# Three token-major projections by 512 columns instead of 256, the feed forward's norm spread over the output projection, and other fill orders in two stages

## The chip, the cores and the metric

The kernel runs on one core of one Trainium2 chip. The metric is the device time of one execution in microseconds (us). Before the change it is 3830.4 us, the median of 3 runs (3830.1 to 3832.64). Engines are named as the profile names them: PE is TensorE's matmul, PEld its weight load, DVE VectorE, ACT ScalarE, POOL GpSimd, SP SyncE, which issues most DMAs.

## The reference

The input is one sequence of 1024 tokens of width 1024, in fp32. Two blocks follow each other:

- The first block: a norm, one wide input projection, and four mixers of width 512 beside each other: latent attention (mla), window pooling, a state-space mixer (ssd) in 8 chunks of 128 tokens, and a linear recurrence (lru). `merged` is the sum of four gated projections of their outputs, and `x = x + merged @ w_out`. Then `x = x + square(relu(rmsnorm(x) @ w_ff1)) @ w_ff2` with 4096 hidden features, then `x = x + (p @ w_ple) * sigmoid(rmsnorm(x) @ w_ple_gate)`, and a norm.
- The second block: a modulated norm, an input projection, gated linear attention (gla) and retention, both in two directions, `x = x + mod * (mixed @ w_out_2)`, a router over 16 experts, each of which takes its best 128 tokens, the experts' feed forward, and a last norm.

In the ssd mixer, for each chunk and each of two groups g of four heads, a masked segment sum over the chunk goes through an exponential, is multiplied with the chunk's `cb` product and then with the inputs; the result is the diagonal part of the output.

## The kernel before

**Products.** Every large product is fp32 as three matmuls: operands are split into a high part (`_hi`, by ACT) and a rest (`_lo`, by DVE; `split`, L93 to L98), and `mm3` (L100 to L106) issues high by high, high by low and low by high for each block of 128 features, into one PSUM accumulator. Where the output stands token-major (128 tokens by n columns), the activations are the stationary operand and the weights stream; a name `mm<-w_hi,m_hi` in the trace is such a matmul (`m` is the merged activation, `hh` a normed one, `a` the feed forward's hidden activation).

**Weights.** `fetch` (L198) loads a weight block in two raw halves through SP's queue and splits each; the high tile and the low tile, 1 MB each, have two buffers each.

**PSUM.** Two pools: 5 accumulators for large products (`ps_mm`) and 3 for the rest (`ps_ax`).

**The order.** Each engine runs one program in order. A framework's scheduler sets it from the order of the code and from what depends on what. Where a stage has little for PE, the code takes pieces of another stage from a queue: `fill(n)` issues the next n pieces. In the ssd stage the queue holds the gate projections (`gates`): a piece there is a third of an accumulation of 24 matmuls of 512 columns, 9, 9 or 6 of them.

**The stages that the change touches:**

- ssd, L408 to L480, from about 322 to 490 us. Per chunk: 6 pieces, transposes (`s_tp`), the `cb` products, and for both groups POOL's product of the mask and the decays (`s_al`, L436), the segment sum on PE (`s_sg`, L440), the exponential on ACT (L442), the product with `cb` on DVE (`s_m`, L443) and the matmuls `s_yd` (L446). Then the off-diagonal part (`s_yo`) and the state (`s_ct`).
- the merge and `w_out`, L786 to L817, from about 1060 to 1343 us, each by halves h of 512 tokens. After a half's merged features are there, `w_out` runs in 4 blocks of 256 columns, 4 token tiles each. For h = 1, the norm of tiles 0 to 3 (`norm_half(0, g_mlp)`, L807) stands ahead of it: per tile a Square with a sum on ACT, a root, a reciprocal and a product on DVE (`n_xn`, L127), 8 transposes (`n_ps`, L117), and two splits.
- the feed forward, 1343 to 2059 us; the norm of tiles 4 to 7 stands ahead of its first group.
- the gated per-layer input (PLE), L908 to L960, 2059 to 2191 us: `w_ple_gate` in 4 blocks of 256 columns per half, beside each the product of p with `w_ple`.
- gla, where the queue gives 2 pieces before each of four states.
- `w_out_2`, L1692 to L1740, 2792 to 2916.5 us: 4 blocks of 256 columns per half; after each token tile's block DVE and POOL update x, ACT takes squares, and a routing item follows: two transposes (`q_t`, L1671), a copy on ACT (`q_xT`, L1673), two matmuls with the router (`q_lgp`, L1677). In the last block the tile's norm is written out too (`q_xn`, ACT L1689).

## Time and profile before

| what | us |
|---|---|
| median of 3 runs | 3830.4 |
| the profiled execution's own time | 3829.97 |
| its span, first to last instruction | 3828.3 |
| PE busy | 3645.7 (95%) |
| DVE busy | 2184.7 (57%) |
| ACT busy | 1595.1 (42%) |
| POOL busy | 618.8 (16%) |

The profile is of one execution. Its span leaves 1.67 us of the execution's time outside. The mean granted TensorE clock is 0.98 of 2.4 GHz; where it is 0.5 the array runs at 1.2 GHz. Matmuls are pipelined: the profile models their ends, so that the busy time of a group of matmuls counts overlap, and the pace of a stream is read from start to start.

### The profile page before, as it was taken

How to read it: one execution, taken by the hardware profiler on the slowest of the kernel's cores; microseconds unless marked ns; L12 is line 12 of the kernel's file. 1: busy time of each engine (PE TensorE's matmuls, PEld its weight loads, DVE VectorE, ACT ScalarE, POOL GpSimd, SP SyncE). 2: the span in 40 equal slices, each digit the busy share in tenths (PEclk: the TensorE clock that was granted, in tenths of full speed). 3: DMA queues.
4: the chain of work that ended last, by engine and by line, in shares of the span. 5: the costliest groups of instructions: out<-in, count | busy, mean ns of one | idle time of the engine just before them, and what ended most of it. 6: DMA issues, size and time to landing. Idle time of an engine off the chain costs nothing.

```text
span 3828.3 us, 50597 instructions
## 1 busy us (share of the span) xinstructions
PE 3645.7 (95%) x19648; PEld 3023.6 (79%) x19648; DVE 2184.7 (57%) x3304; ACT 1595.1 (42%) x2310; POOL 618.8 (16%) x731
## 2 busy tenths in 40 slices
PE   8999899999999899999999999989996999999997
PEld 6787688888779888888888988878985677777775
DVE  5425523333455566555435556575554688877777
ACT  7432243333333222222224656445242566654555
POOL 0002310101122200000000211222331222222111
PEclk9999999999999999999999999999997999999999
DMA  4211111221366423332213252223366799998987
GB/s 124 74 51 53 63 51 57 68 65 51 121 196 184 132 79 93 110 96 92 88 45 105 78 144 65 78 79 113 115 219 237 248 354 364 370 347 325 356 335 267
DMA packets 309037, 583.07 MB, mean 152 GB/s; under 512 B 27342, under 2 KB 211756, under 8 KB 308796
## 3 DMA queue, kind: packets, MB, share of 16 engines
q1 hardware_dynamic: 286508, 509.52, 39.0%
q0 software_dynamic: 22288, 70.31, 5.4%
q8 instruction: 155, 2.54, 0.3%
q14 instruction: 86, 0.70, 0.1%
HBM read 513.66 MB, written 66.09 MB: 151 GB/s over the span
## 4 chain that ended last, share of the span: by engine, by line
PE 68%; DVE 5%; issue 4%; ACT 3%; DMA 3%; POOL 2%; SPq 0%; DVEq 0%; POOLq 0%; ACTq 0%
PE mm L104 13%; PE mm L105 13%; PE mm L106 13%; PE mm L1831 5%; PE mm L1828 5%; PE mm L1829 5%; PE mm L1827 5%; PE sc L604 2%; PE m_o L638 1%; DMA w_raw<-in_w_in_dram 1%; DVE w_lo L96 1%; PE m_pt L629 1%; DMA m_g<-gates 1%; DVE e_lo L1804 1%; PE g_s L1361 1%
## 5 line engine op out<-in xcount | busy, mean ns | idle before, releaser
L104 PE MATMUL mm<-hh_hi,w_hi 128*128 128x512 f32 x1872 | 748.7, 400 | 5.4 <-ACT p_u L321 2.1
L105 PE MATMUL mm<-hh_lo,w_hi 128*128 128x512 f32 x1872 | 738.0, 394 | 0.1
L106 PE MATMUL mm<-hh_hi,w_lo 128*128 128x512 f32 x1872 | 737.1, 394 | 0.5 <-DVE w_lo L96 0.5
L1804 DVE TENSOR_TENSOR e_lo<-e_raw,e_hi 128x1408 fp32r<-128x1408 f32 (+1 forms) x308 | 502.5, 1671 | 59.2 <-ACT e_hi L1803 57.5
L96 DVE TENSOR_TENSOR w_lo<-w_raw,w_hi 128x1024 fp32r<-128x1024 f32 (+4 forms) x284 | 348.9, 1244 | 245.9 <-ACT w_hi L94 244.3
L1803 ACT ACTIVATE e_hi<-e_raw 128x1408 fp32r<-128x1408 f32 (+1 forms) x308 | 408.7, 1373 | 139.7 <-PE mm L1829 67.4
L104 PEld LDWEIGHTS mm<-hh_hi,w_hi 128*128 128x128 f32 x1872 | 354.0, 189 | 81.4 <-issue 5.1
L106 PEld LDWEIGHTS mm<-hh_hi,w_lo 128*128 128x128 f32 x1872 | 353.5, 189 | 77.6 <-issue 2.7
L105 PEld LDWEIGHTS mm<-hh_lo,w_hi 128*128 128x128 f32 x1872 | 354.3, 189 | 71.6 <-issue 3.3
L94 ACT ACTIVATE w_hi<-w_raw 128x1024 fp32r<-128x1024 f32 (+4 forms) x284 | 273.6, 985 | 326.8 <-PE mm L105 177.7
L104 PE MATMUL mm<-w_hi,hh_hi 128*128 128x256 f32 x1152 | 334.4, 291 | 0.0
L105 PE MATMUL mm<-w_lo,hh_hi 128*128 128x256 f32 x1152 | 328.5, 285 | 0.0
L106 PE MATMUL mm<-w_hi,hh_lo 128*128 128x256 f32 x1152 | 327.4, 285 | 0.0
L104 PEld LDWEIGHTS mm<-w_hi,hh_hi 128*128 128x128 f32 x1152 | 221.6, 193 | 4.1 <-issue 0.2
L105 PEld LDWEIGHTS mm<-w_lo,hh_hi 128*128 128x128 f32 x1152 | 222.0, 193 | 2.0 <-issue 1.5
L106 PEld LDWEIGHTS mm<-w_hi,hh_lo 128*128 128x128 f32 x1152 | 221.6, 193 | 0.1
L1827 PE MATMUL mm<-e_hi,e_xh 128*128 128x512 f32 x540 | 208.0, 409 | 0.0
L1828 PE MATMUL mm<-e_lo,e_xh 128*128 128x512 f32 x540 | 203.8, 377 | 0.0
L1829 PE MATMUL mm<-e_hi,e_xl 128*128 128x512 f32 x540 | 203.6, 377 | 0.0
L105 PE MATMUL mm<-w_lo,a_hi 128*128 128x512 f32 x512 | 199.6, 390 | 0.0
L104 PE MATMUL mm<-w_hi,a_hi 128*128 128x512 f32 x512 | 199.6, 390 | 0.0
L106 PE MATMUL mm<-w_hi,a_lo 128*128 128x512 f32 x512 | 199.3, 389 | 0.0
(653 smaller groups left out, 6625.4 us busy)
## 6 DMA issues: line engine op xcount, KB each, us to landing
e_raw<-in_w_exp_down_dram SPq DMA_DIRECT2D x112, 768.0 KB
e_raw<-in_w_exp_gate_dram SPq DMA_DIRECT2D x90, 704.0 KB
e_raw<-in_w_exp_up_dram SPq DMA_DIRECT2D x90, 704.0 KB
w_raw<-in_w_in_dram SPq DMA_DIRECT2D x82, 512.0 KB
w_raw<-in_w_ff_dram SPq DMA_DIRECT2D x64, 512.0 KB
w_raw<-in_w_ada_dram SPq DMA_DIRECT2D x48, 512.0 KB
e_nat<-in_w_exp_up_dram SPq DMA_DIRECT2D x32, 704.0 KB
e_nat<-in_w_exp_gate_dram SPq DMA_DIRECT2D x30, 704.0 KB
```

Source lines behind the costliest of these rows:

```text
L94: S.activation(hi, src, AF.Copy, scale=1.0 if scale is None else scale)
L96: V.tensor_sub(lo, src, hi.bitcast(F32))
L104: P.matmul(ps, ah, bh, start=start and k == 0, stop=False)
L105: P.matmul(ps, ah, bl, start=False, stop=False)
L106: P.matmul(ps, al, bh, start=False, stop=stop and k == nk - 1)
L604: P.matmul(sc[:, b:e], qT[:, h, i * 128:n], kT[:, h, b:e], start=True, stop=e < n)
L1803: S.activation(hi[:, :n], r[:, :n], AF.Copy)
L1804: V.tensor_sub(lo[:, :n], r[:, :n], hi[:, :n].bitcast(F32))
L1827: P.matmul(ps, x[0][:, k], w[0][:, c0:c1], start=k == 0, stop=False)
L1828: P.matmul(ps, x[0][:, k], w[1][:, c0:c1], start=False, stop=False)
L1829: P.matmul(ps, x[1][:, k], w[0][:, c0:c1], start=False, stop=k == last)
L1831: P.matmul(ps, x[2](k), w[:, c0:c1], start=k == 0, stop=k == last)
```

## The change

It has four parts.

1. `w_out`, `w_ple_gate` and `w_out_2` go by 512 columns. Four accumulators of 512 columns are open, one for each token tile; a weight block is 512 columns of four of the eight feature blocks (`quarter`, the same 1 MB). The first quarter passes over all four tiles, then the second one (`wide_tm`). `w_ple` goes by 512 too, and is loaded and split once instead of once per half; p's transposed form is made half by half. After a tile's second pass, x is updated by 512 columns, in PLE the squares too; in `w_out_2` the update and the routing stay at 256 columns, two after each other.
2. The feed forward's norm of tiles 0 to 3 stands inside `w_out` of h = 1 (tiles 0 and 1 behind the second pass of its first 512 columns, tiles 2 and 3 behind the first pass of the last), that of tiles 4 to 7 between the feed forward's first units.
3. In ssd the 6 pieces per chunk stand in three places: 1 ahead of the chunk, 3 between the two groups' segment sums, 2 between the two groups' `s_yd`.
4. In gla the first state of each round has 4 pieces ahead of it instead of 2.

```diff
@@ -240,6 +240,21 @@
...
     H5 = lambda h: slice(h * 512, (h + 1) * 512)
+    def quarter(w_pm, c, b):
+        return fetch(w_pm[:, b * 4:b * 4 + 4, H5(c)], 4, 512)
+    def wide_tm(w_pm, c, x, first=None):
+        ps = [ps_mm() for _ in range(4)]
+        for b in range(2):
+            w = first if first and not b else quarter(w_pm, c, b)
+            for i in range(4):
+                mm3(ps[i], x, w, 4, lambda t, k: t[:, b * 4 + k, i * 128:(i + 1) * 128], lambda t, k: t[:, k, :],
+                    start=b == 0, stop=b == 1)
+                yield i, ps[i] if b else None
@@ -406,7 +421,7 @@
...
             for c in range(NT):
-                fill(6)
+                fill(1)
                 tk = slice(c * 128, (c + 1) * 128)
@@ -430,8 +445,8 @@
...
                     S.activation(bt, p[:, :128], AF.Copy)
-                yd = ps_ax("s_yd")
-                for g in range(2):
+                def segments(g):
                     al = sp.tile([128, 2, 4, 128], F32R, name="s_al4", tag="s_xin", bufs=2)
@@ -441,9 +456,18 @@
...
                     V.tensor_mul(m, m, cbm[:, g, None, :].to_broadcast([128, 4, 128]))
+                    return m
+                yd = ps_ax("s_yd")
+                ms = [segments(0)]
+                fill(3)
+                ms.append(segments(1))
+                for g in range(2):
+                    if g:
+                        fill(2)
                     for r in range(4):
                         h = g * 4 + r
-                        P.matmul(yd[:, h * 64:(h + 1) * 64], m[:, r], xdt[:, h], start=True, stop=True)
+                        P.matmul(yd[:, h * 64:(h + 1) * 64], ms[g][:, r], xdt[:, h], start=True, stop=True)
                 y = sp.tile([128, 8, 64], F32, name="s_y", bufs=2)
@@ -804,17 +828,13 @@
...
                 hT[0] = half()
-                norm_half(0, g_mlp, range(0, 4))
-            for c in range(4):
-                w = fetch(w_out[:, :, c * 256:(c + 1) * 256], KD, 256)
-                ps = [ps_mm()[:, :256] for _ in range(4)]
-                for k0, k1 in ((0, KD - 1), (KD - 1, KD)) if c == 0 else ((0, KD),):
-                    for i in range(4):
-                        mm3(ps[i], m, w, k1 - k0, lambda t, k: t[:, k0 + k, i * 128:(i + 1) * 128],
-                            lambda t, k: t[:, k0 + k, :], start=k0 == 0, stop=k1 == KD)
-                for i in range(4):
-                    xr = xres[:, h * 4 + i, c * 256:(c + 1) * 256]
-                    V.tensor_add(xr, xr, ps[i])
+            for c in range(2):
+                for i, p in wide_tm(w_out, c, m):
+                    if p is not None:
+                        xr = xres[:, h * 4 + i, H5(c)]
+                        V.tensor_add(xr, xr, p)
+                    if h == 1 and (p is None) == (c == 1) and i % 2 == 1:
+                        norm_half(0, g_mlp, [c * 2 + i // 2])
     early.close()
@@ -857,10 +877,11 @@
...
                 w = [wf1(0), wf1(2)]
-                norm_half(1, g_mlp, range(4, 8))
-                for h in range(2):
-                    for q in range(4):
-                        act[q, h] = ff1(w[q // 2], q, h)
+                for q in range(4):
+                    act[q, 0] = ff1(w[q // 2], q, 0)
+                    norm_half(1, g_mlp, [4 + q])
+                for q in range(4):
+                    act[q, 1] = ff1(w[q // 2], q, 1)
                 fill(1)
@@ -906,19 +927,16 @@
...
     with tc.tile_pool(name="ple", bufs=1) as pl:
-        pT = (pl.tile([128, 2, T], F32R, name="pT_hi"), pl.tile([128, 2, T], F32R, name="pT_lo"))
-        pg = lambda c: fetch(w_pg[:, :, c * 256:(c + 1) * 256], KD, 256)
-        w = pg(0)
-        def ple_w(c):
-            r = pl.tile([128, 2, 256], F32, name="w2_raw", bufs=2)
-            t = pl.tile([128, 2, 256], F32R, name="w2_hi", bufs=2), pl.tile([128, 2, 256], F32R, name="w2_lo", bufs=2)
-            SP.dma_start(r, w_ple[:, :, c * 256:(c + 1) * 256])
-            split(t[0], t[1], r)
-            return t
-        w2 = ple_w(0)
-        for h in range(2):
+        w = quarter(w_pg, 0, 0)
+        w2 = pl.tile([128, 2, D], F32R, name="w2_hi"), pl.tile([128, 2, D], F32R, name="w2_lo")
+        for c in range(2):
+            r = raw_half(2, 512)
+            SP.dma_start(r, w_ple[:, :, H5(c)])
+            split(w2[0][:, :, H5(c)], w2[1][:, :, H5(c)], r)
+        def p_half(h):
+            pT = pl.tile([128, 2, 512], F32R, name="pT_hi"), pl.tile([128, 2, 512], F32R, name="pT_lo")
             pin = [pl.tile([128, 256], F32, name="p_in", bufs=4) for _ in range(4)]
@@ -926,7 +944,10 @@
...
                     P.transpose(p[:, i * 128:(i + 1) * 128], pin[i][:, j::2], ident)
-                split(pT[0][:, j, H5(h)], pT[1][:, j, H5(h)], p)
+                split(pT[0][:, j], pT[1][:, j], p)
+            return pT
+        pT = p_half(0)
         norm_half(1, g_ple, range(4, 8))
@@ -939,25 +960,23 @@
...
         for h in range(2):
-            ss = pl.tile([128, 2, 4, 4], F32, name="f_ss", bufs=2)
+            ss = pl.tile([128, 2, 4, 2], F32, name="f_ss", bufs=2)
             s1 = pl.tile([128, 2, 4], F32, name="f_s1", bufs=2)
-            for c in range(4):
-                if c or h:
-                    w, w2 = pg(c), ple_w(c)
-                for i in range(4):
-                    _, tk = tok(i)
+            if h:
+                pT = p_half(1)
+            for c in range(2):
+                for i, p in wide_tm(w_pg, c, h3[h], w if c == 0 and h == 0 else None):
+                    if p is None:
+                        continue
+                    gt = pl.tile([128, 512], F32, name="pl_g", bufs=3)
+                    S.activation(gt, p, AF.Sigmoid)
                     p = ps_mm()
-                    mm3(p[:, :256], h3[h], w, KD, lambda t, k: t[:, k, tk], lambda t, k: t[:, k, :])
-                    gt = pl.tile([128, 256], F32, name="pl_g", bufs=3)
-                    S.activation(gt, p[:, :256], AF.Sigmoid)
-                    p = ps_mm()
-                    r = slice(h * 512 + i * 128, h * 512 + (i + 1) * 128)
-                    mm3(p[:, :256], pT, w2, 2, lambda t, k: t[:, k, r], lambda t, k: t[:, k, :])
-                    V.tensor_mul(gt, p[:, :256], gt)
-                    xr = xres[:, h * 4 + i, c * 256:(c + 1) * 256]
-                    G.tensor_add(xr, xr, gt)
+                    mm3(p, pT, w2, 2, lambda t, k: t[:, k, i * 128:(i + 1) * 128], lambda t, k: t[:, k, H5(c)])
+                    V.tensor_mul(gt, p, gt)
+                    xr = xres[:, h * 4 + i, H5(c)]
+                    (V if h and c else G).tensor_add(xr, xr, gt)
                     if h == 1:
-                        squares(gt, xr, c * 256, 256, ss[:, :, i, c])
+                        squares(gt, xr, c * 512, 512, ss[:, :, i, c])
             if h == 0:
@@ -1327,7 +1346,7 @@
...
                 nla = decays(*steps[s + 1]) if s < 3 else None
-                fill(2)
+                fill(4 if s == 0 else 2)
                 states(d, h, la)
@@ -1396,7 +1415,6 @@
     w_out2 = I["w_out_2"][0].rearrange("(j p) n -> p j n", p=128)
-    wo = lambda c: fetch(w_out2[:, :, c * 256:(c + 1) * 256], KD, 256)
@@ -1512,7 +1530,7 @@
...
                     until("rg1")
-                    ahead = [wo(0), wo(1)]
+                    ahead = [quarter(w_out2, 0, b) for b in range(2)]
                     oT = [half(), half()]
@@ -1702,35 +1720,34 @@
...
         wait = []
-        for c in range(4):
-            w = ahead.pop(0) if ahead else wo(c)
-            def part(p, i, k0, k1):
-                mm3(p, oT[h], w, k1 - k0, lambda t, k: t[:, k0 + k, i * 128:(i + 1) * 128],
-                    lambda t, k: t[:, k0 + k, :], start=k0 == 0, stop=k1 == KD)
-            ps = [ps_mm()[:, :256] for _ in range(4)] if h == 0 and c == 0 else None
-            if ps:
+        for c in range(2):
+            w = ahead if ahead else [quarter(w_out2, c, b) for b in range(2)]
+            ahead = None
+            ps = [ps_mm() for _ in range(4)]
+            def part(i, k0, k1):
+                mm3(ps[i], oT[h], w[k0 // 4], k1 - k0, lambda t, k: t[:, k0 + k, i * 128:(i + 1) * 128],
+                    lambda t, k: t[:, k0 % 4 + k, :], start=k0 == 0, stop=k1 == KD)
+            split_at = (4, 7) if h == 0 and c == 0 else (4,)
+            for k0, k1 in zip((0,) + split_at[:-1], split_at):
                 for i in range(4):
-                    part(ps[i], i, 0, KD - 1)
+                    part(i, k0, k1)
             for i in range(4):
-                if ps:
-                    p = ps[i]
-                    part(p, i, KD - 1, KD)
-                else:
-                    p = ps_mm()[:, :256]
-                    part(p, i, 0, KD)
-                t = rp.tile([128, 256], F32, name="o_t", bufs=3)
-                V.tensor_mul(t, p, m2[:, c * 256:(c + 1) * 256])
-                xr = x1[i][:, c * 256:(c + 1) * 256]
-                (V if c == 3 and h else G).tensor_add(xr, xr, t)
-                S.activation(t, xr, AF.Square, accum_out=ss[:, i, c:c + 1])
-                wait.append(route(h, i, c, xr))
-                if len(wait) > 3:
-                    next(wait.pop(0))
-                if len(wait) > 2:
-                    next(wait[0])
-                if c == 3:
+                part(i, split_at[-1], KD)
+                for b in range(2):
+                    q = c * 2 + b
+                    t = rp.tile([128, 256], F32, name="o_t", bufs=3)
+                    V.tensor_mul(t, ps[i][:, b * 256:(b + 1) * 256], m2[:, q * 256:(q + 1) * 256])
+                    xr = x1[i][:, q * 256:(q + 1) * 256]
+                    (V if c and h else G).tensor_add(xr, xr, t)
+                    S.activation(t, xr, AF.Square, accum_out=ss[:, i, q:q + 1])
+                    wait.append(route(h, i, q, xr))
+                    if len(wait) > 3:
+                        next(wait.pop(0))
+                    if len(wait) > 2:
+                        next(wait[0])
+                if c == 1:
                     rstd(i)
...
                         finish(x1[i], rs[:, i:i + 1], h * 4 + i)```

On PE, in the third ssd chunk, before, this stands between the chunk's transposes and the next pieces; `mm` are the matmuls of the gate pieces:

```order
L413 MATMUL s_tp<-ident,s_x 128x128 x4
L426 MATMUL s_cb<-s_x 128x128 x2
L440 MATMUL s_sg<-s_al_2554,s_sgr 128x512 x2
L440 MATMUL s_sg<-s_al_2566,s_sgr 128x512 x2
L104 MATMUL mm<-hh_hi,w_hi 128x512
L430 MATMUL s_bt<-ident,s_x 128x128
L105 MATMUL mm<-hh_lo,w_hi 128x512
...
L106 MATMUL mm<-hh_hi,w_lo 128x512
L446 MATMUL s_yd<-s_xdt,s_m 128x64 x8
L451 MATMUL s_yo<-s_st_2222,s_x 128x512
```

Both segment sums stand together, and 6 matmuls of 512 columns are between them and the 8 `s_yd`. On PE in the same chunk after the change:

```order
L441 MATMUL s_cb<-s_x 128x128 x2
L455 MATMUL s_sg<-s_al_2508,s_sgr 128x512 x2
L104 MATMUL mm<-hh_hi,w_hi 128x512
...
L106 MATMUL mm<-hh_hi,w_lo 128x512
L455 MATMUL s_sg<-s_al_2544,s_sgr 128x512 x2
L470 MATMUL s_yd<-s_xdt,s_m 128x64 x4
L104 MATMUL mm<-hh_hi,w_hi 128x512
...
L106 MATMUL mm<-hh_hi,w_lo 128x512
L470 MATMUL s_yd<-s_xdt,s_m 128x64 x4
L475 MATMUL s_yo<-s_st_2222,s_x 128x512
```

Now 24 such matmuls are between the first segment sum and the second, and 15 between the second one and its `s_yd`; 9 are left ahead of the chunk.

On PE at the start of `w_out` of h = 1, before (the `n_ps` are the transposes of tile 0's norm, `mm<-w,m` the projection, which has 51 matmuls of 256 columns ahead of them):

```order
L106 MATMUL mm<-hh_hi,w_lo 128x512
...
L104 MATMUL mm<-w_hi,m_hi 128x256
L105 MATMUL mm<-w_lo,m_hi 128x256
L106 MATMUL mm<-w_hi,m_lo 128x256
L117 MATMUL n_ps<-ident,n_xn 128x128 x8
L104 MATMUL mm<-w_hi,m_hi 128x256
```

and after, at the same place:

```order
L106 MATMUL mm<-hh_hi,w_lo 128x512
L104 MATMUL mm<-w_hi,m_hi 128x512
L105 MATMUL mm<-w_lo,m_hi 128x512
L106 MATMUL mm<-w_hi,m_lo 128x512
...
L117 MATMUL n_ps<-ident,n_xn 128x128 x8
L104 MATMUL mm<-w_hi,m_hi 128x512
```

72 matmuls of 512 columns stand ahead of tile 0's transposes now; between those and the next tiles' there are 24, 26 and 22.

On PE in `w_out_2`, at the end of the first 512 columns of h = 0, after the change; the routing items were 24 matmuls of 256 columns apart before, with 4 or 5 matmuls between an item's `q_t` and its `q_lgp`:

```order
L1689 MATMUL q_t<-ident,x_21779 128x128 x2
L1695 MATMUL q_lgp<-w_r_21750,q_xT 128x16 x2
L1689 MATMUL q_t<-ident,x_21780 128x128 x2
L1695 MATMUL q_lgp<-w_r_21750,q_xT 128x16 x2
L1689 MATMUL q_t<-ident,x_21780 128x128 x2
L104 MATMUL mm<-w_hi,hh_hi 128x512 x2
L1695 MATMUL q_lgp<-w_r_21750,q_xT 128x16 x2
L1689 MATMUL q_t<-ident,x_21781 128x128 x2
```

Here transposes and router matmuls of one item follow each other with little or nothing between; further on 3 matmuls of 512 columns stand in one gap and 9 in the next, in turn.

## Rows read from the trace of the kernel before

**Rows 1.** The page's busy times.

```profile
PE 3645.7 (95%) x19648; PEld 3023.6 (79%) x19648; DVE 2184.7 (57%) x3304; ACT 1595.1 (42%) x2310; POOL 618.8 (16%) x731
```

**Rows 2.** PE groups by form: line, operation, shapes, count | busy, mean ns | idle before.

```profile
L104 PE MATMUL mm<-w_hi,a_hi 128*128 128x512 f32 x512 | 199.6, 390 | 0.0
L104 PE MATMUL mm<-w_hi,m_hi 128*128 128x256 f32 x256 | 73.3, 286 | 0.0
```

**Rows 3.** Timeline of PE, end of merge to end of w_out, h = 0 (start, duration).

```profile
1145.64 0.39 PE L106 MATMUL mm<-hh_hi,w_lo 128*128 128x512 f32 x1
...
1147.23 0.28 PE L104 MATMUL mm<-w_hi,m_hi 128*128 128x256 f32 x1
...
1193.30 0.40 PE L104 MATMUL mm<-hh_hi,w_hi 128*128 128x512 f32 x1
```

**Rows 4.** Timeline of PE in the feed forward's second product.

```profile
1507.16 0.39 PE L104 MATMUL mm<-w_hi,a_hi 128*128 128x512 f32 x1
...
1511.92 0.39 PE L104 MATMUL mm<-w_hi,a_hi 128*128 128x512 f32 x1
```

**Rows 5.** Waits of PE: total us, times, longest.

```profile
PE s_yd L446 <- DVE s_m L443: 19.8, 10, 3.6
...
PE n_ps L117 <- DVE n_xn L127: 10.9, 2, 10.5
```

**Rows 6.** Timeline of an ssd chunk, 364 to 371 us, all engines.

```profile
364.83 1.09 ACT L442 ACTIVATE s_m<-s_sg 128x512 f32<-128x512 f32 x2 [0.94 <-PE s_sg L440]
...
365.46 5.20 DVE L443 TENSOR_TENSOR s_m<-s_m,s_cbm 128x512 f32<-128x512 f32 x2
...
365.75 3.75 POOL L436 TENSOR_TENSOR s_al<-triu,s_ap 128x1024 fp32r<-128x1024 f32 x2
...
370.12 0.55 PE L446 MATMUL s_yd<-s_xdt,s_m 128*128 128x64 f32 x3 [3.43 <-DVE s_m L443]
```

**Rows 7.** Windows, ssd and its half-clock piece: us, busy of PE, PEld, DVE, ACT, POOL, PEclk.

```profile
321.95:490.00 168.05, 147.01 (x680) 112.61 (x679) 88.42 (x115) 41.81 (x76) 56.97 (x50) 0.95 0.17 56
...
371.30:374.80 3.50, 3.50 (x11) 2.27 (x11) 0.98 (x2) 0.00 (x0) 0.00 (x0) 0.51 0.00 0
```

**Rows 8.** Timeline of the first norm in w_out, h = 1.

```profile
1293.63 0.63 ACT L94 ACTIVATE m_hi<-m_acc 128x512 fp32r<-128x512 f32 x1 [9.00 <-POOL m_acc L741]
...
1294.29 0.69 DVE L98 SCALAR_TENSOR_TENSOR m_lo<-m_acc,m_hi 128x512 fp32r<-128x512 f32 x1 [1.22 <-ACT m_hi L94]
...
1298.95 1.97 PE L117 MATMUL n_ps<-ident,n_xn 128*128 128x128 f32 x8 [10.49 <-DVE n_xn L127]
```

**Rows 9.** Window behind that wait, columns as in Rows 7.

```profile
1298.95:1303.30 4.35, 4.35 (x21) 4.35 (x22) 1.70 (x4) 2.52 (x5) 0.00 (x0) 0.51 0.36 117
```

**Rows 10.** Timeline of PE, norms of the feed forward's second half.

```profile
1355.65 1.12 PE L117 MATMUL n_ps<-ident,n_xn 128*128 128x128 f32 x8
...
1360.81 1.13 PE L117 MATMUL n_ps<-ident,n_xn 128*128 128x128 f32 x8
```

**Rows 11.** Timeline of PE in gla: the two waits that have more cover now.

```profile
2360.89 0.63 PE L1305 MATMUL g_ktp<-ident,g_la 128*128 128x128 f32 x4 [1.47 <-DVE g_la L1299]
...
2363.82 1.99 PE L1312 MATMUL g_ct<-g_v,ho_y 128*128 128x256 f32 x8 [1.00 <-ACT ho_y L1307]
```

**Rows 12.** Windows of PLE and w_out_2, columns as in Rows 7.

```profile
2059.00:2191.00 132.00, 127.25 (x1042) 125.15 (x1041) 77.50 (x113) 86.17 (x179) 33.17 (x37) 1.00 0.35 108
...
2792.00:2916.50 124.50, 120.44 (x1007) 118.69 (x1005) 52.51 (x137) 56.18 (x134) 34.80 (x55) 0.99 0.55 184
```

**Rows 13.** Timeline of the last routing items of w_out_2.

```profile
2911.68 1.15 ACT L1689 ACTIVATE q_xn<-x,q_rs 128x1024 f32<-128x1024 f32 x1 [0.23 <-DVE q_rs L110]
...
2913.53 0.38 ACT L1673 ACTIVATE q_xT<-q_t 128x256 f32<-128x256 f32 x1 [0.70 <-PE q_t L1671]
...
2913.90 0.42 ACT L1727 ACTIVATE o_t<-x 128x256 f32<-128x256 f32 x1
...
2913.97 0.62 PE L1677 MATMUL q_lgp<-w_r,q_xT 128*128 128x16 f32 x4 [0.53 <-ACT q_xT L1673]
```

## The prediction, on record before the changed kernel ran

> **What bounds the kernel now.** I read the busy times first: PE is busy for 3645.7 of the span, 95%, and no other engine comes near [rows 1]. So time is won only in two ways: fewer or quicker matmuls, or fewer holes in PE's program. Second came PE's groups by form, for the matmuls that the change replaces, and PE's timeline beside them, since a mean duration and a pace are not the same thing here. A matmul of 256 columns is booked with 286 ns and one of 512 with 390 [rows 2]. In the timeline seven matmuls of 512 columns start within 1147.23 - 1145.64 = 1.59 us, 0.227 each, and the 384 of 256 columns of `w_out`'s first half within 1193.30 - 1147.23 = 46.07 us, 0.1200 each, without a hole [rows 3]. The feed forward's second product, which has the same layout as the changed ones (activations stationary, weights streaming by 512), starts 21 in 4.76 us: 0.2267 [rows 4]. Third came PE's waits: among the largest are 19.8 us for the ssd product `s_m` and 10.9 us for a norm [rows 5]; both are in stages that the change touches.
>
> **Part 1, the pace.** One matmul of 512 columns replaces two of 256: 2 x 0.1200 - 0.2270 = 0.0130 us saved for each pair (0.2270 lies between the two rows, [rows 3, 4]). Each of the three projections has 2 halves x 4 blocks x 4 tiles x 24 = 768 matmuls, so 384 pairs; the product with `w_ple` has 192, so 96 pairs. That is 3 x 384 + 96 = 1248 pairs, and 1248 x 0.0130 = 16.2 us saved. Bounds: if the new stream is as quick as the feed forward's fastest start distance, 0.2267, 16.6; if a pair saves only half of it, because a weight load or an eviction shows, 8.
>
> The Trainium skill, TensorE: Matmul & The Clock Gate, section Back-to-back issue gap, gives an isolated matmul N divided by 2.4 GHz plus 2.5 ns. By that, a pair would save only the fixed 2.5 ns, and an estimate of the whole part from this page is 1248 x 2.5 ns = 3.1 us in place of 16.2. The trace does not agree in the fixed part: 0.1200 and 0.2270 differ by 0.1070 for 256 more columns, which leaves 0.013 per matmul [rows 3].
>
> DMA bytes stay equal, a quarter is as large as a block was, and each lasts 48 x 0.227 = 10.9 us on PE against 96 x 0.120 = 11.5 before, so the weight splits keep their cover. `w_ple` is split once instead of per half; ACT and DVE are not late there, so I cost that at nothing.
>
> **Part 2, the norm in the output projection.** Before, the 8 transposes of tile 0 wait 10.49 us for `n_xn`, because ACT is held by `m_hi` until 1293.63, and the norm's Square stands behind it [rows 8]. Behind the wait PE runs at 0.51 for 4.35 us [rows 9], which costs about 4.35 x 0.49 = 2.1 us. Together 12.6. Ahead of that wait stood 51 matmuls, 51 x 0.120 = 6.1 us, so PE had 6.1 + 10.5 = 16.6 us until `n_xn` was there. Now 72 matmuls of 512 stand there, 72 x 0.227 = 16.3 us; 0.3 is left. `m_lo` of the last feature block, ready at 1294.98 [rows 8], is needed by the second pass: PE begins at 1298.95 - 16.6 = 1282.35, the first pass takes 48 x 0.227 = 10.9, three more blocks 9 x 0.227 = 2.0, so it is asked for at 1295.3. That holds by 0.3 us. The other tiles' norms have 24, 26 and 22 matmuls, 5.0 us or more, of cover. In the feed forward the same chain went with 18: the transposes of two tiles start 5.16 us apart, which is 1.1 of transposes and 18 x 0.227 = 4.1, so nothing was waited for [rows 10]; now it has 24 there. I take 12 us saved; the ends are 12.6, and 9 if the last merge or a norm slips by a us or two in each of the first tiles.
>
> **Part 3, ssd.** The gap of 3.43 us before `s_yd` comes from DVE: two products `s_m` take 5.20 us together while POOL makes the next chunk's two `s_al` beside them, 3.75 us [rows 6]; the exponentials on ACT take 0.55 each. Over the stage PE waits 19.8 us for it [rows 5]. The mean clock is 0.95 of 168.05 us, since PE falls to 0.51 behind such a gap and is busy through that piece [rows 7]: 0.05 x 168 = 8.4 us lost. Together 28.2 us. Now the first `s_m` has 24 x 0.227 = 5.4 us of cover and the second 15 x 0.227 = 3.4 plus four `s_yd` of 0.14, 3.9. What the second needs: an exponential, 0.55, and a product beside at most one `s_al`, 1.9 + 0.7 = 2.6, together 3.2. So the cover holds, with 0.7 to spare. I take 24 us saved, leaving 4 for chunks in which the POOL queue comes late (half a us each). Ends: 28; and 10, if both `s_al` still stretch the second product: 0.55 + 4.6 - 3.9 = 1.2 us x 8 chunks = 10 wait, and the clock's 8.4 stay lost.
>
> The Trainium skill, SBUF — State Buffer, section Who interferes with whom, says that a VectorE instruction with two SBUF inputs and a GpSimd instruction that reads SBUF exclude each other for a whole instruction, and the one that starts first goes on. The row does not agree on who goes on: DVE began at 365.46, POOL at 365.75, and still both products took 5.20 [rows 6]. By the page a product that has begun would take no stretch at all, and the gain would be the full 28.
>
> **Part 4, gla.** Two waits of 1.47 and 1.00 us [rows 11] get 7 and 18 more matmuls of 256 columns ahead of them, 7 x 0.120 = 0.8 us and 18 x 0.120 = 2.2: the first keeps some 0.6, the second goes. I take 2 us saved (0 to 2.5): the pieces come out of later filler, and the larger waits of this stage have the same cover as before.
>
> **What is added.** In PLE PE lost 132.00 - 127.25 = 4.75 us before [rows 12]. The norm's transposes of two tiles now have 17 and 16 matmuls of cover instead of the 18 with which the chain just goes in the feed forward; DVE and ACT have more beside it, so I take 2 us (0 to 5).
> In `w_out_2` the routing items come in pairs. An item that has nothing between its transposes and its router matmuls waits 0.53 us for ACT's copy [rows 13]; four stand so at the end of the first 512 columns, 2.1 us, and up to one more comes from copies that queue behind a Square. In the last 512 columns ACT has for each tile two copies of 0.38, two Squares of 0.42 and `q_xn` of 1.15 [rows 13], 2.75 us, and PE has 12 x 0.227 = 2.72; before it was 1.95 against 24 x 0.120 = 2.88. ACT becomes level with PE there, and the tail behind the last matmul carries one item more. I take 5 us in all (0 to 10; the ends are four bare items hidden, and every tile late by ACT's read of its sums).
>
> **The sum**, from the profiled execution's 3829.97 us: -16.2 - 12 - 24 - 2 + 2 + 5 = -47.2, which gives 3782.8. That execution lies 0.4 under the median of the runs shown, which makes 3783.2 of it; the forecast is 3783 us. The stages in between keep their order, and the experts at the end are not touched.
>
> **Rivals.**
> 1. The second `s_m` is still late: gain of 10 instead of 24 in ssd, 3797 us. For it: POOL's two `s_al` may run back to back if POOL is late with the state's product. Against: each is released by its own segment sum, and these now stand 5.4 us apart.
> 2. The ssd wait only moves: with 9 matmuls ahead of a chunk instead of some 40, the transposes or the segment sum wait for the chunk before, and the 24 are given back: 3807 us. For it: the same work of DVE, 88.42 of 168.05 us [rows 7], is now to fit into fewer us. Against: DVE would be at 88 of 140, and the state is needed late in the chunk.
> 3. No pace is won: each new matmul takes what two took, 0.2400, because four open accumulators swing through the banks. 3783 + 16.2 = 3799 us. Against: the feed forward's rows [rows 4]. The Trainium skill's gap rule, cited above, lies near this one.
> 4. The booked durations count: 2 x 286 - 390 = 182 ns a pair [rows 2], 1248 x 0.182 = 227 us, so 3783 + 16 - 227 = 3572 us. Against: a pair cannot save more than what its starts take, 0.240 [rows 3].
> 5. Slower: routing in `w_out_2` becomes serial. Each item goes PE, ACT, PE; if the copy stands behind a Square (0.42), and `q_xn` (1.15), it comes 0.38 + 0.42 + 1.15 = 1.95 us late, and 32 items x 1.95 = 62 us. Without the 3 us counted for bare items that gives 3783 - 3 + 62 = 3842. It decides from about 1.6 us an item on, (3830 - 3780) / 32. For it: pairs, and ACT level with PE. Against: the tail's item waits 0.53 with a Square and `q_xn` near it [rows 13], and most of the 32 keep matmuls between.
>
> **How the numbers follow.** Forecast 0.71, rival 1 0.10, rival 2 0.06, rival 3 0.05, rival 4 0.02, rival 5 0.06. Adding the ends, the likeliest case reaches from 3829.97 - 16.6 - 12.6 - 28 - 2.5 = 3770 to 3802 (the ends don't meet all at once). The range should hold the rivals 1 to 3, too: 3768 to 3812. The measurement of this kernel tells about 0.2%, 7.7 us, from no change. All cases but the fifth are faster than that; the fifth, near its deciding point, and several bad ends at once could come out within it: faster 0.88, same 0.06, slower 0.06.
>
> **What would show it.** Starts of `mm<-w_hi,m_hi` at 512 columns 0.227 apart; no wait over 1 us before `s_yd`, and the clock at 1.00 between 322 and 465 us; the first `n_ps` of `w_out`, h = 1, with a wait under 1 us; ssd shorter by 24 us, `w_out` of h = 1 by 17. Wrong would be: new waits of PE for `s_tp`, `s_ct` or `q_xT` of more than 5 us in sum, or a pace of 0.235 or more.

## The result, and the profile after

The changed kernel takes 3784.97 us, the median of 4 runs (3781.26 to 3791.93), against 3831.52 of the kernel before beside it: a ratio of 0.988, 95% interval 0.9863 to 0.9897. The forecast was 3783 us in a range of 3768 to 3812. The profiled execution took 3785.97 us.

The page after, its head and its busy times:

```profile
span 3784.3 us, 47941 instructions
PE 3625.3 (96%) x18400; PEld 2953.1 (78%) x18400; DVE 2168.9 (57%) x3266; ACT 1587.4 (42%) x2257; POOL 614.5 (16%) x707
```

PE has 1248 matmuls less, yet only 20.4 us less of busy time [rows 1]; the span is 44.0 us shorter, so the other 23.6 are holes that closed. Reading in both traces where the same instruction of PE starts gives this table by stages, in us:

| stage | before | after | difference | foreseen |
|---|---|---|---|---|
| start to the last `s_yt` of ssd | 487.68 | 460.63 | -27.1 | -24 |
| to the start of `w_out`, h = 0 | 659.55 | 663.34 | +3.8 | 0 |
| `w_out`, h = 0 | 46.07 | 43.52 | -2.55 | -2.5 |
| merge, h = 1 | 88.81 | 87.05 | -1.8 | 0 |
| `w_out`, h = 1 | 61.07 | 49.17 | -11.9 | -14.5 |
| feed forward | 715.27 | 714.75 | -0.5 | 0 |
| PLE | 132.22 | 125.32 | -6.9 | -4.2 |
| to the first `g_ktp` of gla | 152.13 | 149.58 | -2.6 | 0 |
| first to last `g_ktp` | 188.27 | 195.11 | +6.8 | -2 |
| to the last `r_ct` of retention | 255.97 | 249.24 | -6.7 | 0 |
| to the last `q_lgp` of `w_out_2` | 129.14 | 136.14 | +7.0 | 0 |
| router, to the first gathered rows | 46.49 | 43.70 | -2.8 | 0 |
| experts, to PE's last instruction | 846.68 | 847.35 | +0.7 | 0 |

The pace, in PE's timeline after (start, duration): the first matmul of `w_out`, h = 0, and the first behind it.

```profile
1123.97 0.39 PE L104 MATMUL mm<-w_hi,m_hi 128*128 128x512 f32 x1
...
1167.49 0.39 PE L104 MATMUL mm<-hh_hi,w_hi 128*128 128x512 f32 x1
```

192 matmuls in 43.52 us are 0.2267 each, what the feed forward's rows had said [rows 4].

PE's waits after (total us, times, longest); `s_yd` and the norm's `n_xn` led this list among the stages that changed [rows 5]:

```profile
PE g_ktp L1324 <- DVE g_la L1318: 11.1, 3, 6.6
...
PE q_lgp L1695 <- ACT q_xT L1691: 3.5, 6, 0.8
...
PE s_yd L470 <- DVE s_m L458: 1.3, 1, 1.3
...
PE mm L104 <- DVE m_g L763: 1.1, 1, 1.1
```

19.8 us became 1.3. In one ssd chunk after, all engines:

```profile
338.28 0.60 ACT L457 ACTIVATE s_m<-s_sg 128x512 f32<-128x512 f32 x1 [1.92 <-PE s_sg L455]
338.34 1.89 POOL L451 TENSOR_TENSOR s_al<-triu,s_ap 128x1024 fp32r<-128x1024 f32 x1 [1.13 <-PE s_sg L455]
338.91 1.87 DVE L458 TENSOR_TENSOR s_m<-s_m,s_cbm 128x512 f32<-128x512 f32 x1 [4.22 <-ACT s_m L457]
...
342.35 1.00 PE L470 MATMUL s_yd<-s_xdt,s_m 128*128 128x64 f32 x8
```

One `s_al` beside one `s_m`: the product is done at 340.78, 0.55 us behind POOL, and `s_yd` comes at 342.35 without a wait. The same stretch as windows (us, busy of PE, PEld, DVE, ACT, POOL, clock, DMA share, GB/s), to be held against [rows 7]:

```profile
313.09:460.63 147.54, 142.50 (x699) 110.92 (x698) 83.71 (x121) 49.38 (x81) 60.39 (x51) 1.00 0.22 69
```

The clock is 1.00 on the mean of the stage, against 0.95. At the start of `w_out`, h = 1, after:

```profile
1263.68 1.35 DVE L763 SCALAR_TENSOR_TENSOR m_g<-m_g,mm 128x512 f32<-128x512 f32 x2 [4.91 <-DMA m_g<-gates]
1264.42 0.50 PE L104 MATMUL mm<-w_hi,m_hi 128*128 128x512 f32 x1 [1.14 <-DVE m_g L763]
...
1273.20 1.06 PE L117 MATMUL n_ps<-ident,n_xn 128*128 128x128 f32 x8
```

The wait of 10.49 us [rows 8] is gone; the norm's transposes wait for nothing. A wait of 1.14 us is new at this place: some 36 matmuls into the stage, where the fourth accumulator is opened, PE waits for DVE to read a merge product out of it, and DVE had waited for that product's gates.

### The profile page after: what moved, and what is told of

The parts are those of the page before. It is cut to its first block, busy times and chain, and to the rows that moved or that the text cites. A ratio compares the mean times of both kernels' runs of the same rounds, so it can differ in the third digit from the quotient of the medians.

```text
span 3784.3 us, 47941 instructions
## 1 busy us (share of the span) xinstructions
PE 3625.3 (96%) x18400; PEld 2953.1 (78%) x18400; DVE 2168.9 (57%) x3266; ACT 1587.4 (42%) x2257; POOL 614.5 (16%) x707
## 3 DMA queue, kind: packets, MB, share of 16 engines
q8 instruction: 145, 2.38, 0.3%
## 4 chain that ended last, share of the span: by engine, by line
PE 68%; DVE 6%; issue 4%; DMA 3%; ACT 3%; POOL 2%; SPq 0%; DVEq 0%; POOLq 0%; ACTq 0%
PE mm L104 13%; PE mm L106 13%; PE mm L105 13%; PE mm L1848 5%; PE mm L1845 5%; PE mm L1846 5%; PE mm L1844 5%; PE sc L628 2%; PE m_o L662 1%; DVE w_lo L96 1%; DMA m_g<-gates 1%; PE m_pt L653 1%; DMA w_raw<-in_w_in_dram 1%; PE g_s L1380 1%; DVE e_lo L1821 1%
## 5 line engine op out<-in xcount | busy, mean ns | idle before, releaser
L104 PE MATMUL mm<-hh_hi,w_hi 128*128 128x512 f32 x1872 | 750.4, 401 | 5.4 <-ACT p_u L336 2.1
L105 PE MATMUL mm<-hh_lo,w_hi 128*128 128x512 f32 x1872 | 737.1, 394 | 0.2 <-DVE hh_lo L96 0.2
L106 PE MATMUL mm<-hh_hi,w_lo 128*128 128x512 f32 x1872 | 736.0, 393 | 0.5 <-DVE w_lo L96 0.5
L94 ACT ACTIVATE w_hi<-w_raw 128x1024 fp32r<-128x1024 f32 (+4 forms) x278 | 270.4, 995 | 359.0 <-PE mm L105 191.1
L104 PEld LDWEIGHTS mm<-hh_hi,w_hi 128*128 128x128 f32 x1872 | 353.6, 189 | 81.4 <-issue 5.7
L106 PEld LDWEIGHTS mm<-hh_hi,w_lo 128*128 128x128 f32 x1872 | 353.2, 189 | 77.5 <-issue 1.7
L105 PEld LDWEIGHTS mm<-hh_lo,w_hi 128*128 128x128 f32 x1872 | 354.0, 189 | 72.1 <-issue 4.3
L104 PE MATMUL mm<-w_hi,hh_hi 128*128 128x256 f32 (+1 forms) x896 | 291.6, 326 | 0.3 <-ACT w_hi L94 0.3
L105 PE MATMUL mm<-w_lo,hh_hi 128*128 128x256 f32 (+1 forms) x896 | 285.7, 319 | 0.0
L106 PE MATMUL mm<-w_hi,hh_lo 128*128 128x256 f32 (+1 forms) x896 | 284.7, 318 | 0.0
L105 PE MATMUL mm<-w_lo,a_hi 128*128 128x512 f32 x512 | 199.6, 390 | 0.0
L104 PE MATMUL mm<-w_hi,a_hi 128*128 128x512 f32 x512 | 199.6, 390 | 0.0
L106 PE MATMUL mm<-w_hi,a_lo 128*128 128x512 f32 x512 | 199.3, 389 | 0.0
L104 PEld LDWEIGHTS mm<-w_hi,hh_hi 128*128 128x128 f32 x896 | 173.3, 194 | 14.3 <-issue 0.8
L105 PEld LDWEIGHTS mm<-w_lo,hh_hi 128*128 128x128 f32 x896 | 173.3, 193 | 10.3 <-issue 1.0
L106 PEld LDWEIGHTS mm<-w_hi,hh_lo 128*128 128x128 f32 x896 | 173.3, 193 | 10.1
```

The source lines that it names most:

```text
L94: S.activation(hi, src, AF.Copy, scale=1.0 if scale is None else scale)
L104: P.matmul(ps, ah, bh, start=start and k == 0, stop=False)
L105: P.matmul(ps, ah, bl, start=False, stop=False)
L106: P.matmul(ps, al, bh, start=False, stop=stop and k == nk - 1)
```

## The experiments

Each run was timed beside the kernel before; "after" is the changed kernel. Stages are read as in the table.

**The ssd part undone** in the changed kernel.

```diff
-                fill(1)
+                fill(6)
...
-                ms = [segments(0)]
-                fill(3)
-                ms.append(segments(1))
...
-                    if g:
-                        fill(2)
```

> The changed kernel with the ssd part undone: six gate pieces ahead of a chunk, both segment sums together, as before. Theory (cover: the second product s_m now lies behind 15 matmuls, and the clock no longer falls): the stage, from its first to its last transposes s_tp to s_yt, goes back from 147.5 to about 165.7 us, PE waits about 20 us for s_m again, five half-clock pieces come back, and the whole is 3785 + 24 to 27 = 3809 to 3812 us. Rival (the wait only moved to later stages, whose gaps grew by as much): no more than 10 us above 3785.

3811.37 us (3810.19 to 3814.75), 26.4 above 3784.97. Its PE waits:

```profile
PE s_yd L461 <- DVE s_m L458: 19.8, 10, 3.6
```

The stage ends 28.0 us later, and every later stage stays within 2.2 us: the part is worth what its own stage shows.

**The norm ahead of `w_out` again**, in the changed kernel.

```diff
                 hT[0] = half()
+                norm_half(0, g_mlp, range(0, 4))
...
-                    if h == 1 and (p is None) == (c == 1) and i % 2 == 1:
-                        norm_half(0, g_mlp, [c * 2 + i // 2])
...
```

> The changed kernel with the feed forward's norm put ahead of w_out of h = 1 again, and that of the second half ahead of the feed forward's first units; w_out stays by 512 columns. Theory (the norm stands behind the last merged feature on ACT and PE waits for it): a wait of 5 to 10.5 us for n_xn comes back, with some 3 to 4 us at half clock, 3785 + 8 to 12 = 3793 to 3797. Rival (the 512-column order alone covers the norm, since more of PE's work stands ahead of it): no more than 3 us above 3785. The pace of w_out's first half stays 0.227 us a matmul by either.

3799.25 us (3794.03 to 3801.58), 14.3 above, a little more than expected; `w_out`, h = 1, takes 59.22 us, 10.0 more. Its PE waits:

```profile
PE n_ps L117 <- DVE n_xn L127: 11.3, 2, 10.9
```

So the 512-column order alone covers nothing of it. The other 4 us are spread over stages before and behind it, none of them more than 1.9 us, in the size of what differs between executions (below).

**`w_out_2` by 256 columns again**, the rest as changed (the before's loop, with `wo(c)`, in place of the quarters).

> The changed kernel with w_out_2 by 256 columns as before, one routing item after every 24 matmuls. The stage from the last r_ct to the last q_lgp took 129.1 us before and 136.1 after. Theory (the pairs of routing items cost more than the pace gives: waits for the copy, the clock's fall behind them, and small matmuls that no longer overlap): the stage goes back to about 129 us, and the whole is 3785 - 7 = 3778. Rival (the stage was longer through the clock's fall that the earlier gaps of the retention heads caused, wherever these lie): the stage stays at 134 or more plus 5 us for the lost pace, and the whole is 3785 to 3790.

3783.22 us (3781.33 to 3790.17). The stage took 130.92 us, 5.2 less than 136.14, but the router behind it 2.8 more (its wait for gathered rows). The stage goes most of the way to the theory's 129. The whole does not reach its 3778, and can't be told from no change. The stage's difference is larger than its spread: it takes 132.6 to 136.1 us in the six traces that hold the changed `w_out_2`, and 128.8 to 130.9 in the five that hold it by 256 columns. The router behind it differs with it, 43.6 to 45.0 us in the nine traces in which `w_out_2` goes by 512 columns in any form, and 46.2 to 46.6 in the five by 256. So the -2.8 of the table belongs to the change too, and gives back part of what the stage costs; why is not shown.

**Routing by 512 columns.**

```diff
-                for b in range(2):
-                    q = c * 2 + b
...
+                t = rp.tile([128, 512], F32, name="o_t", bufs=2)
+                V.tensor_mul(t, ps[i], m2[:, H5(c)])
...
+                wait.append(route(h, i, c, xr))
```

> The changed kernel with the routing and the update in w_out_2 by 512 columns too: one item for each token tile and 512 columns, four transposes, one copy, four router matmuls; 16 items in place of 32, with 12 matmuls between them. Theory (pairs of items cost some 12 us in the stage against its pace): waits for the copy fall from 3.5 to about 1.5 us, one half-clock piece goes, the stage is 124 to 128 us in place of 136, the whole 3773 to 3778. Rival (the time is lost to the gaps ahead of w_out_2 and not to the items): the stage stays above 133 us, the whole within 3 us of 3785.

3784.83 us (3780.58 to 3786.34), the stage 133.45. The theory misses: waits for the copy fall to 2.7 us only, since the first item still stands bare (1.36 us), and the half-clock piece behind it stays. The rival's two numbers are met, but its reason is not shown by that: with the same code ahead of `w_out_2`, the form by 256 columns took 130.92.

**The same, the first items deferred** into the next block's first pass.

```diff
                     part(i, k0, k1)
+                    if h == 0 and c == 1:
+                        step(0)
```

> As the run with routing by 512 columns, and the items of the first 512 columns of h = 0 are begun in the next block's first pass, behind 12 matmuls each, instead of between 3 matmuls each. Theory (bare items at that place make PE wait and the clock fall): at most one item there stays bare, the wait at this place falls from 1.9 to about 1 us, the half-clock piece behind it goes (1.7 us), the stage from the last r_ct to the last q_lgp falls from 133.5 to 130 us, the whole 3776 to 3782. Rival (the piece comes from the wait for weights and from the retention gaps ahead of it): the stage stays at 133 or more, the whole at 3783 to 3787.

3782.52 us (3776.95 to 3785.56), the stage 131.64. The scheduler still put one item bare in front of that block (waits for the copy 3.2 us); the half-clock piece is 3.4 us in place of 6.8. Neither theory is settled by it: the same `w_out_2` takes 129.49 us in the run of the parts together below, so 1.8 us between two forms can't be told from chance.

**The changed kernel again.**

> The changed kernel again, beside the others on one chip, for its spread: 3785 us within 5 by either theory, and each stage within 1.5 us of its first profile if stages are what differ between kernels; where a stage differs by more from one execution to the next, differences of that size between kernels aren't told apart.

3788.57 us (3784.55 to 3790.04). Stages differ by up to 2.0 us from the first profile (PLE: 127.36 against 125.32). Over all 14 traces the stretch from the last `s_yt` to `w_out`, h = 0, whose code is the same in every kernel, takes 658.0 to 664.8 us, and the one from PLE to the first `g_ktp` 148.1 to 152.1 (148.8 to 152.1 in the four kernels with 2 pieces in gla). So the +3.8 and -2.6 of the table are of the size of what one execution differs from the next, and I draw nothing from them.

**The ssd part alone**, on the kernel before.

> The kernel before with the ssd part of the change alone. Theory (the parts add up, each from its own stage): the stage from the first s_tp to the last s_yt falls from 165.7 to about 147.5 us, no wait over 1.5 us before s_yd, the whole 3830 - 24 to 27 = 3803 to 3806. Rival (the gain needs the other parts, or later stages give it back, since the gate pieces then end at another place): 3812 or more.

3798.92 us (3795.18 to 3801.45), 30.8 below the 3829.71 beside it; the stage ends at 459.44, 28.2 earlier. That is more than expected, and nearly all of it lies within the stage.

**`s_al` on DVE**, on the kernel before, one letter:

```diff
-                    G.tensor_mul(al, triu[:, None, None, :].to_broadcast([128, 2, 4, 128]),
+                    V.tensor_mul(al, triu[:, None, None, :].to_broadcast([128, 2, 4, 128]),
```

> The kernel before with one edit: the product of mask and decays, s_al, on DVE in place of POOL, so that nothing of it runs on POOL beside the product s_m; the pieces stay where they were. It adds two instructions of 128x1024 to DVE for each chunk. Theory (s_m is slow because POOL reads beside it): each s_m takes 0.7 us in place of 0.6 to 4.6, the largest wait before s_yd falls from 3.6 to about 1.5 us, that sum from 19.8 to under 12, some half-clock pieces go, the whole 3830 - 8 to 18 = 3812 to 3822. Rival (s_m waits for its inputs, and its long rows are waiting time and not contention): s_m keeps rows over 2 us, the waits stay at 18 us or more, the whole at 3830 or above, since DVE has more to do.

3796.98 us (3792.78 to 3801.41), 32.7 below: the pieces stand where they stood, DVE runs 16 instructions of 20.5 us more, and the gain is nearly twice the upper end of what was expected. The stage ends at 459.21, 28.5 earlier. DVE's groups in this run (count | busy, mean ns):

```profile
L436 DVE TENSOR_TENSOR s_al<-triu,s_ap 128x1024 fp32r<-128x1024 f32 x16 | 20.5, 1282 | 0.1
...
L443 DVE TENSOR_TENSOR s_m<-s_m,s_cbm 128x512 f32<-128x512 f32 x16 | 10.7, 709 | 0.2
```

The same product in the kernel before:

```profile
L443 DVE TENSOR_TENSOR s_m<-s_m,s_cbm 128x512 f32<-128x512 f32 x16 | 36.0, 2290 | 0.9 <-ACT s_m L442 0.7
```

On the mean, 0.709 against 2.290 us is the price of POOL's neighbour. It is more than what was added: DVE is busy for 2175.8 us in this run and was for 2184.7. Row by row, in the kernel before, the 16 products take 0.68 or 0.69 us where nothing of POOL's runs beside them (6), 2.38 beside one `s_al` (6), and 4.26 to 4.82 where two `s_al` go ahead of them (4). A chunk in the run with `s_al` on DVE:

```profile
357.31 1.09 ACT L442 ACTIVATE s_m<-s_sg 128x512 f32<-128x512 f32 x2 [0.94 <-PE s_sg L440]
357.94 1.51 DVE L443 TENSOR_TENSOR s_m<-s_m,s_cbm 128x512 f32<-128x512 f32 x2
...
359.02 1.89 PE L446 MATMUL s_yd<-s_xdt,s_m 128*128 128x64 f32 x16
```

Both products are done at 359.45, 2.1 us after the first exponential began, and PE's 6 matmuls between the segment sums and `s_yd` cover what the first needs; no wait for `s_m` is left in the stage, nor a half-clock piece. The ordering of the pieces hides the contention, this edit removes it.

**`s_al` on DVE in the changed kernel** (the same edit).

> The changed kernel with s_al on DVE and the spread gate pieces kept. Theory (both take away the same waits, so they don't add): 3785 less 0 to 4, s_m at 0.7 us each, the largest wait before s_yd under 1 us. Rival (they add, since the changed kernel still waits in the stage and its s_m are 1.35 us): 3778 or less, the stage's end at 456 or earlier.

3782.32 us (3780.92 to 3789.35). `s_m` takes 0.710 us, no wait for it is left, the stage ends 3.5 us earlier. They hardly add: the stage is 30.5 us shorter than before with both, 27.1 with the order alone and 28.5 with `s_al` on DVE alone.

**Gla as before**, in the changed kernel: `fill(2)`.

> The changed kernel with 2 pieces ahead of each state in gla, as before. The stretch from the first g_ktp to the last r_ct took 244.2 us before and 244.4 after. Theory (pieces put ahead of the first state are missing later, and the larger wait grows by what the two small ones lose): the stretch from the first to the last g_ktp goes from 195 back to 188 us, that from there to the last r_ct grows by as much, the whole stays within 3 us of 3785. Rival (the part saves its 2 us): the whole 3787 and the stretch to the last r_ct 2 us longer.

3785.79 us (3783.26 to 3787.96). First to last `g_ktp` 188.38 us, 6.7 less; from there to the last `r_ct` 252.92, 3.7 more. The theory holds in direction; on the whole time the part gives nothing. The two stretches together take 440.5 to 444.2 us in the four traces with 2 pieces, and 442.4 to 448.4 in the ten with 4: if the part does anything to them, it costs some 3 us.

**The parts together**: ssd's order as before with `s_al` on DVE, `w_out` and PLE as changed, and `w_out_2` deferred by 512, or wholly by 256.

> The parts put together: the changed kernel with the ssd part undone and s_al on DVE, and with w_out_2's routing by 512 columns, its first items deferred. Theory (without POOL beside it s_m takes 0.7 us, so the old order has cover enough): the ssd stage ends at 459 to 460 us in place of 460.6, no wait for s_m over 1 us, the whole 3776 to 3782, from the deferred run's 3782.5 less 1 to 5. Rival (the pieces between the segment sums are still needed, since DVE now also carries s_al): waits of some us in ssd, the whole 3785 or more.

3777.19 us (3771.62 to 3780.18), ratio to before 0.9865 (0.9847 to 0.9882).

> As the run that puts the parts together, with w_out_2 wholly by 256 columns as before. Theory (w_out_2 by 512 columns is worth its 5 us of pace less what its routing costs; with 16 items it is 1 to 3 us the better): this is 1 to 3 us above the other, its stage from the last r_ct to the last q_lgp 131 us. Rival (the stage's gain is eaten by the wait for the gathered rows behind the router): both within 1 us.

3773.96 us (3772.41 to 3776.82), 0.9856 (0.984 to 0.9873). The first is in its expected range, and its ssd stage ends at 457.06 without a wait for `s_m`; of the second the sign was wrong: it is 3.2 us below the first and not above, and the ranges overlap. No run of either lies within the changed kernel's 8 runs (3781.26 to 3791.93), so both beat the kernel before and the changed one, and the one with the lower median leaves out part 3 and what part 1 does to `w_out_2` (part 4 is still in it).

## Why the prediction was right, and where a step was off

- **Pace.** Right: 0.2267, and 2.55 us for `w_out` of h = 0, the half in which nothing else changed. Rivals 3 and 4 fall. The fixed part between the two widths is 0.013 us a matmul, as the rows had shown, and not the 2.5 ns that the Trainium skill gives (TensorE: Matmul & The Clock Gate, Back-to-back issue gap).
- **Norm.** Right in mechanism: the wait of 10.9 us that comes back with the norm's old place is the proof. One reading was wrong, in the prediction and in the list of PE's order ahead of it: the transposes that waited were the second tile's; the first tile's stood just ahead of `w_out`. That puts 1.05 us of transposes into the stage after that are outside it before, so -11.9 stands for -13.0 against -14.5. Most of the other 1.5 is the wait of 1.14 us for the accumulator: in the three of ten traces with this order that have no such wait the stage takes 47.73 to 48.12 us in place of 49.17, and 49.64 where it is longest, 1.92. I had checked whether `m_lo` is there in time, and not whether the fourth of five accumulators is free: opening four at once asks for the last merge's own accumulator. (The 17 us that the prediction names among its signs for this stage does not follow from its sum, which has 2.5 and 12.)
- **ssd.** Right, and the likeliest value a little low: the clock's pieces all went, and the wait fell to 1.3 us, in the first chunk. That is over the 1 us that the prediction gave as a sign. Rival 1 and rival 2 fall by the waits: what is new or longer in the stage otherwise (`s_yt`, `s_bt`, and `s_yd` for `s_cbm`) is some 2.4 us in sum. Behind it, contention is shown and not only argued, by the run with `s_al` on DVE. By the page (the Trainium skill, SBUF — State Buffer, Who interferes with whom) two such instructions exclude each other; the rows agree, with 0.55 us from POOL's end to DVE's. The prediction read from its row that the first to start does not go on, and that was a misreading: when DVE's row begins at 365.46 POOL is not idle, another product of its own is running until 365.81.

```profile
364.75 1.06 POOL L421 TENSOR_TENSOR s_xdd<-s_xdt,s_ecs 128x512 f32<-128x512 f32 x1
```

In the kernel before and in the changed one every `s_m` that is held began while a POOL instruction was running. The rows show besides that the held time is booked as DVE's, and that a waiting product may be passed: here two `s_al` go ahead of it. After the change, at 366.85, a product waits for `s_xdd` alone, takes 0.76 us and goes ahead of the next `s_al`, which is the longer for it (2.35 us, against 1.89 in the chunk shown above):

```profile
367.02 2.35 POOL L451 TENSOR_TENSOR s_al<-triu,s_ap 128x1024 fp32r<-128x1024 f32 x1
```

What decides who comes next, no run here shows.

- **Gla.** Failed: 2 us foreseen, nothing found. The step that failed is that the larger waits keep their cover and the pieces come out of later filler for nothing: the two small waits went, and one of 1.24 us with them, but the next `g_ktp` waits 1.74 now, the largest wait grew from 5.25 to 6.61, and the pieces were missing in the next stretch.
- **PLE.** -6.9 for -4.2. PE's waits for its norms grew from 1.98 us to 4.76, 2.8 for the 2 foreseen. Waits for p and `w_ple` fell from 2.56 to 0.77, which I had not counted. So the holes are 5.57 us against 4.75, 0.8 more. With 6.4 for the pace that makes -5.6; the other 1.3 is open.
- **`w_out_2`.** The step that was mis-sized: I added 5 us and took 5.0 off for the pace. Against the run with the 256-column form, in the same surroundings, the stage is 5.2 us longer, so what was added is 10.2 (10.0 by the means of the six and the five traces above). The timeline after, at the end of the first 512 columns:

```profile
2778.37 0.62 PE L1695 MATMUL q_lgp<-w_r,q_xT 128*128 128x16 f32 x4 [0.82 <-ACT q_xT L1691]
...
2779.74 0.62 PE L1695 MATMUL q_lgp<-w_r,q_xT 128*128 128x16 f32 x4 [0.48 <-ACT q_xT L1691]
```

The bare items wait 0.48 to 0.82 us each, near what was foreseen (0.53). Not foreseen was the clock behind them; a window of the changed kernel, then one of the run with 256 columns at the same place (columns as above):

```profile
2781.80:2788.60 6.80, 6.49 (x24) 5.33 (x23) 2.96 (x6) 2.97 (x6) 0.00 (x0) 0.50 0.43 117
```

```profile
2783.00:2790.00 7.00, 7.00 (x63) 7.00 (x63) 3.40 (x8) 3.42 (x9) 2.49 (x2) 1.00 0.71 225
```

A piece of 6.8 us or more stands at this place in all six traces with the changed `w_out_2`, and in none of the five with 256 columns. In this trace another covers the stage's last 3.4 us, from 2870.5 on, and one of 6.8 us ahead of the projection, from 2757.9, has its like with 256 columns. So 17.0 us of the stage run at half clock against 6.8, which costs some 4.8 us, the holes in these pieces left out. PE's holes in the stage are 8.8 us against 5.4, 3.4 more. And where the clock is full, the router's small matmuls start 0.096 us one behind another against 0.090, 0.5 more. Together 8.7 of 10.2; the rest is open. Rival 5 is the direction in which it went, at a sixth of its price.

The upper end of the likeliest case, 3802, leaves out the terms that are added: the ends as listed come to 3818.

The sum came out near since the misses cancel, and that is luck: ssd and PLE gave 6 us more than foreseen, `w_out_2`, gla and `w_out` of h = 1 some 12 less, and the other stages 3 more, the router among them.

## What to carry to other kernels

A stretched row on one engine beside a busy neighbour is a place to ask which of the two could run elsewhere: moving one product from POOL to DVE, which then ran 16 instructions more and was busy for less, gave as much as reordering a stage around the wait. Before counting a wider output as a gain, read the pace from start to start, and look at what used to stand between the narrow pieces: here the routing lost its cover. Opening more accumulators at once also moves the point at which the stage before must have let go of them.

## What the runs showed of the hardware that was not expected

- A DVE product of two operands in SBUF, 128x512, takes 0.68 or 0.69 us with nothing of POOL's beside it, 2.38 beside one `s_al`, and 4.26 to 4.82 where two `s_al` go ahead of it; it ends 0.55 us behind the POOL instruction that it waited for.
- PE fell to 0.50 at 2781.8 behind four bare routing items. Their single waits were 0.20, 0.82, 0.48 and 0.58 us, 2.1 us in sum since 2776; no wait there was long.
- The router's matmuls of 16 columns start 0.090 us apart among matmuls of 256 columns and, at full clock, 0.096 where they stand in pairs of items.
